# Opening sums added in pairs, the last projection step reordered by bank, the first transposes of attention moved behind one more tile

## The chip, the core and the metric

The kernel runs on one core of one Trainium2 chip. The metric is device time in microseconds of one execution. Three runs of the kernel before gave 907.13, 908.06 and 908.67 us, median 908.06. The core has five engines that run side by side: TensorE (PE in the profile, its weight loads PEld), VectorE (DVE), ScalarE (ACT), GpSimd (POOL) and SyncE (SP, which issues nearly all transfers here).

## What is computed

A trunk of two layers over 512 tokens of 1024 channels, in float32, with a final RMSNorm. Each layer normalises its input, scales and shifts it by values that come from a conditioning vector `c`, mixes tokens, and adds the result back:

```
h = rmsnorm(x, norm_g[i]) * (1.0 + scale) + shift
y = even_mixer(...) if i == 0 else odd_mixer(...)
x = x + (1.0 + gate) * y
```

The change lies in layer 0. There one projection of `h` gives pool channels, `q`, `k`, `v` and a gate. `q`, `k`, `v` feed 16 heads of 64 channels of stick-breaking attention, strictly causal and without a softmax:

```
z = q k^T / 8
log_fail = where(causal, -softplus(z), 0)
after = reverse cumulative sum of log_fail, minus log_fail
a = where(causal, exp(log_sigmoid(z) + after), 0)
o = a v
```

The pool channels go through a causal sliding mean and a small matrix. Both branches are multiplied by SiLU(gate) and projected back.

## The kernel before

**Layout.** Activations lie with channels on the 128 partitions and tokens along the row: `x` is eight tiles of 128x512. Float32 products are made of three passes: each operand is split into a rounded part (`hi`) and a remainder (`lo`), and TensorE adds hi x hi, lo x hi and hi x lo in one PSUM bank (`mm3`, lines 189 to 193). The split is a copy on ScalarE (line 60) and a subtraction on VectorE (line 61). Weights come in units of 512 KB: `load_upto` (line 71) issues their transfers on SyncE into three buffers, `split_upto` (line 78) splits them into three more, and `next_unit` (line 92) hands them out in turn and works two units ahead.

**Banks.** PSUM has eight banks, in two pools: three for projection tiles (`pm`, tile names `m` and `av`) and five for everything else (`pz`, names `z` and `zb`).

**Who orders the work.** For TensorE and SyncE the order of the program text holds throughout (line 498). In `start()` it holds for ScalarE, VectorE and GpSimd too (line 666); elsewhere a scheduler orders those three by readiness and its own costs, and it may put an instruction of later text into a gap of an ordered stretch. It also gives out buffers and banks, by which is free first.

**The opening, `start()` (lines 543 to 660).** Eight matmuls of zeros in bfloat16 (`warm_up(8)`, line 564) are followed by two products of `deps` that start the banks of the token sums with a small constant, and by two products that spread `silu(c)` over the partitions (`cbc`). Then each of the eight `x` tiles is squared, seven on ScalarE and the last on VectorE (lines 574 to 579), and `colsum` (line 142) sums each half of each square over the partitions by a product with ones: 16 sums, each of them two instructions on TensorE. After twelve more warm-up matmuls come the reciprocal root on ScalarE (line 616), its refinement on VectorE (`newton`), and then a loop over the eight channel tiles `k`. In each step VectorE and ScalarE make `hh[k]` and `hl[k]` from `x[k]`, VectorE makes two dot products of `silu(c)` with rows of the conditioning weights (`ada_dot`, line 110, from a ring of four buffers that SyncE refills), the weight unit is split, and TensorE adds to eight banks at once: four of `v` (`pv`, a block of 128 tokens each, lines 656 and 657) and four of `q`, `k` and the first gates (`pq`, lines 658 and 659). A step is three passes over these eight banks:

```
for n, (h, w) in enumerate(((hh, whi), (hl, whi), (hh, wlo))):
    for p, c in zip(pv, tok):
        mm(p, h[:, c], w[:, :512], start=f and n == 0, stop=l and n == 2)
    for p, c in zip(pq, col):
        mm(p, w[:, c], h, start=f and n == 0, stop=l and n == 2)
```

so all eight banks of the last step are complete only near its end.

**After the opening (`layer0`, lines 662 to 681).** `qk_post` (line 313) copies and splits `q` and `k` out of their banks, `v_post` (line 410) does so for `v`, and `silu_ps` (line 210: a sigmoid on ScalarE, a multiply on VectorE) makes the gates `sga` and `sgp`. Each frees its bank. The order of these on ScalarE and VectorE is the scheduler's.

**The loop over pairs of heads (lines 704 to 773).** `self.seq` lists projection tiles (`mtile`, line 195: 24 matmuls of 512 columns): first `u`, then for each later pair `q`, `k`, `ga`, `u`, `gp`. Between the tiles stand the parts of attention of the pair before: `z` (`attn_z`, line 340: scores on TensorE, two sigmoids on ScalarE, masks on GpSimd, scans on VectorE, and one long multiply on VectorE at line 370), `tr` (`attn_t`, line 373: ten transposes on TensorE, then a split), `av` (`attn_av`, line 389: the product with `v`). For the first pair, `u` is followed by `z(0,0)`, the `q` tile by `z(0,1)` and `tr(0,0)`, the `k` tile by `av(0,0)` and `tr(0,1)`, the `ga` tile by `z(1,0)`.

Of the kernel before, what the change touches and what calls it, by code (L numbers as in the profile page):

```python
# [8 lines left out]
F32R = mybir.dt.float32r  # L9
AF = mybir.ActivationFunctionType  # L10
ALU = mybir.AluOpType
# [3 lines left out]
DVE = mybir.EngineType.DVE  # L15
# [22 lines left out]
class Trunk:  # L38
# [504 lines left out]
    def start(self):  # L543
# [15 lines left out]
        def warm_up(n):  # L559

            for _ in range(n):
                mm(warm, self.zero[:, :P], self.zero, start=True, stop=True)

        warm_up(8)

        ps = [self.zbank()[:, :256] for _ in range(2)]
        for p in ps:
# [6 lines left out]
        for k in range(KT):  # L574
            sq = sqs[k // 2][:, k % 2]
            if k == KT - 1:
                nc.vector.tensor_tensor(out=sq, in0=self.x[k], in1=self.x[k], op=ALU.mult)
            else:
                self.square(k, full, sq)
            for p, sl in zip(ps, halves):  # L580
                self.colsum(p, sq[:, sl], False, k == KT - 1)
        warm_up(12)
        nc.sync.dma_start(self.cst, io["cst"])
        ring = self.ap.tile([P, 4, 1024], F32, tag="vs", name="ring")
# [41 lines left out]
        for k in range(KT):  # L626
            self.load_upto(k + 1)
            u = self.units[k]
            whi = self.wp.tile([P, 1024], F32R, tag="whi", name="whi", bufs=3)
            wlo = self.wp.tile([P, 1024], F32R, tag="wlo", name="wlo", bufs=3)  # L630
            if k:
                t = self.h_scale(0, k, rstd, full)
                dot(0, k)
                nc.scalar.copy(out=whi, in_=u["raw"])
                self.h_hi(0, k, t, full)
                dot(1, k + 1)
                self.h_lo(0, k, t, full)
            else:
                self.h_hi(0, 0, t[:, ha], ha)
                nc.scalar.copy(out=whi[:, :512], in_=u["raw"][:, :512])  # L640
                self.h_hi(0, 0, t[:, hb], hb)
                nc.scalar.copy(out=whi[:, 512:], in_=u["raw"][:, 512:])
                self.h_lo(0, 0, t[:, ha], ha)
                self.h_lo(0, 0, t[:, hb], hb)
            nc.vector.tensor_tensor(out=wlo, in0=u["raw"], in1=whi.bitcast(F32), op=ALU.subtract)
            if k == 0:
                dot(1, 1)
            self.split_done = self.used = k + 1
            load(1, k + 2), load(0, k + 2)
            self.load_upto(k + 3)  # L650
            f, l = k == 0, k == KT - 1
            tok = [slice(tb * P, (tb + 1) * P) for tb in range(4)]
            col = [slice(512 + i * P, 512 + (i + 1) * P) for i in range(4)]
            hh, hl = self.hh[k], self.hl[k]
            for n, (h, w) in enumerate(((hh, whi), (hl, whi), (hh, wlo))):
                for p, c in zip(pv, tok):
                    mm(p, h[:, c], w[:, :512], start=f and n == 0, stop=l and n == 2)  # L657
                for p, c in zip(pq, col):
                    mm(p, w[:, c], h, start=f and n == 0, stop=l and n == 2)  # L659
        return pv, pq  # L660

    def layer0(self):
        nc, io = self.nc, self.io
        self.plan_l0()
        self.plan_l1()
        with self.tc.manual_schedule(engines={ACT, DVE, POOL}):
            pv, pq = self.start()
        self.vs = self.ap.tile([P, 4, 1024], F32R, tag="vs", name="vs")

        self.kl = {}  # L670
        for e, z in (("e", slice(64, P)), ("o", slice(0, 64))):
            self.kl[e] = self.ap.tile([P, S], F32R, tag="kl" + e, name="kl" + e)
            nc.vector.memset(self.kl[e][z].bitcast(F32), 0.0)
        self.qk_post(pq[0], "q")
        self.qk_post(pq[1], "k")
        for tb in range(2):
            self.v_post(pv[tb], tb)
        sga = {0: self.silu_ps(pq[2], "sga")}
        for tb in range(2, 4):
            self.v_post(pv[tb], tb)  # L680
        sgp0 = self.silu_ps(pq[3], "sgp")

        self.ada_rest = [(0, 2, k) for k in range(KT)] + [(1, pt, k) for pt in range(3) for k in range(KT)]
        ya, yp, pin, sgp = {}, {}, {}, {self.POOLS[0]: sgp0}
# [2 lines left out]
        def tr(p, par):  # L687
            st["a"] = self.attn_t(st.pop(("s", p, par)))

        def av(p, par):  # L690
            if par == 0:
                st["yt"] = self.t512("yt", bufs=1)
            aps = self.attn_av(2 * p + par, st["a"])
            self.av_post(par, aps, st["yt"])
            if par == 1:
                t = self.t512("t")
                nc.vector.tensor_tensor(out=t, in0=st["yt"], in1=sga.pop(p), op=ALU.mult)
                ya[p] = self.ytile()
                self.hilo(ya[p][0], ya[p][1], t)

        def z(p, par):
            st[("s", p, par)] = self.attn_z(par)

        p = 0
        for kind, j in self.seq:
            if kind == "q":
# [2 lines left out]
                if j == 1:  # L709
                    z(0, 1)  # L710
                self.qk_post(ps, "q")
                tr(j - 1, 0)
            elif kind == "k":
                self.qk_post(self.mtile(), "k")
                av(j - 1, 0)
                tr(j - 1, 1)
            elif kind == "pg":
                yp[2 * j], yp[2 * j + 1] = self.pool_group(
                    j, (pin[2 * j], pin[2 * j + 1]), (sgp[2 * j], sgp[2 * j + 1])
# [2 lines left out]
                    tr(7, 0)  # L722
            elif kind == "ga":
                sga[j] = self.silu_ps(self.mtile(), "sga")
                z(j, 0)
            elif kind == "u":
                pin[j] = self.pool_u(self.mtile(), j)
# [139 lines left out]
def _layout(inp):  # L867
# [11 lines left out]
    sel = np.concatenate([w0[:, :3072], w0[:, 4096:]], axis=1)  # L879
    a["w0m"] = mt(sel, 40)  # L880
    a["w0s"] = np.concatenate(
        [v[:, :512], w0[:, 1024:1152], w0[:, 2048:2176], w0[:, 5120:5248], w0[:, 4864:4992]], axis=1
    ).reshape(KT, P, 1024)
    a["w0v"] = v[:, 512:].reshape(4, 2, P, 512).transpose(0, 2, 1, 3).reshape(4, P, 1024)
    wo = lambda w: w.reshape(16, P, 8, P).transpose(2, 1, 0, 3)
# [39 lines left out]
```

## Time and profile before

| what | value |
|---|---|
| median of three runs | 908.06 us |
| the profiled execution | 907.16 us |
| its span, first to last instruction | 905.5 us |
| mean granted TensorE clock | 0.989 |
| busy: TensorE, its weight loads | 881.9 us (97%), 737.8 us (81%) |
| busy: VectorE, ScalarE, GpSimd | 573.1 us (63%), 354.1 us (39%), 52.1 us (6%) |
| chain that ended last, by engine | TensorE 91%, VectorE 6%, ScalarE 1% |
| memory traffic | 106.69 MB, mean 118 GB/s |

The span leaves out what lies around the first and last instruction. A busy share is a mean over the whole span; the opening, the hand-over to attention and the end have other limits than the long stretch of projection tiles between them. The granted clock is a share of full speed: 1.00 is 2.4 GHz and 0.50 is 1.2 GHz, and a number between them is a stretch with both. A matmul's busy time overlaps with the next one's, so the pace of a row of matmuls is read from their starts.

### The profile page before, as it was taken

The numbers are of one execution on the slowest core, as the hardware profiler recorded it, in microseconds if no ns is written. First come the engines' busy times: TensorE is split into PE (matmuls) and PEld (weight loads), VectorE is DVE, ScalarE is ACT, GpSimd is POOL, SyncE is SP. The second block draws the span as 40 slices with busy tenths as digits, with TensorE's granted clock in tenths as the row PEclk, the third lists the DMA queues.
The fourth block names the chain that finished last, engine by engine and source line by source line (L and its number), as shares of the span: only waits on it lengthen the run. The fifth ranks groups of instructions, "written<-read, shape, count | busy, mean of one in ns | idle before, by whom it ended". The sixth has DMA issues, their size and how long they took to land.

```text
span 905.5 us, 10821 instructions
## 1 busy us (share of the span) xinstructions
PE 881.9 (97%) x4187; PEld 737.8 (81%) x4188; DVE 573.1 (63%) x815; ACT 354.1 (39%) x551; POOL 52.1 (6%) x104
## 2 busy tenths in 40 slices
PE   8988999999999999999999999999999999999995
PEld 5767888888888888888998888888888888888884
DVE  5977889788978688596675445555434444444445
ACT  5355655556322546564443222222112222222331
POOL 0002112012000012020000000000000000000002
PEclk9998999999999999999999999999999999999997
DMA  8851122224677321113512333333332222332202
GB/s 305 282 204 45 39 94 70 82 71 140 227 260 285 100 82 59 59 58 127 165 48 96 129 124 117 117 117 117 104 105 93 93 93 93 101 109 93 93 24 93
DMA packets 30725, 106.69 MB, mean 118 GB/s; under 512 B 3409, under 2 KB 3537, under 8 KB 30674
## 3 DMA queue, kind: packets, MB, share of 16 engines
q1 hardware_dynamic: 30386, 105.48, 34.4%
q8 instruction: 33, 0.54, 0.2%
q10 hardware_dynamic: 288, 0.52, 0.2%
q14 instruction: 18, 0.15, 0.0%
HBM read 103.90 MB, written 2.10 MB: 117 GB/s over the span
## 4 chain that ended last, share of the span: by engine, by line
PE 91%; DVE 6%; ACT 1%; issue 1%; DVEq 0%; POOL 0%; ACTq 0%; POOLq 0%
PE m L191 25%; PE m L192 25%; PE m L193 25%; PE zb L657 2%; PE z L384 2%; PE av L397 2%; PE m L659 2%; PE zb L143 1%; DVE f L368 1%; PE z L354 1%; PE z L353 1%; PE zb L778 1%; PE zb L777 1%; PE zb L779 1%; PE zb L192 1%
## 5 line engine op out<-in xcount | busy, mean ns | idle before, releaser
L60 ACT CAST whi<-raw 128x1024 fp32r<-128x1024 f32 (+1 forms) x137 | 142.8, 1043 | 426.4 <-PE m L192 324.9
L191 PE MATMUL m<-hh,whi 128*128 128x512 f32 x768 | 301.8, 393 | 6.1 <-DVE sga L213 5.5
L192 PE MATMUL m<-hl,whi 128*128 128x512 f32 x768 | 299.9, 391 | 0.0
L193 PE MATMUL m<-hh,wlo 128*128 128x512 f32 x768 | 299.7, 390 | 0.0
L61 DVE TENSOR_TENSOR wlo<-raw,whi 128x1024 fp32r<-128x1024 f32 (+1 forms) x137 | 165.2, 1207 | 124.6 <-ACT whi L60 117.4
L191 PEld LDWEIGHTS m<-hh,whi 128*128 128x128 f32 x768 | 144.9, 189 | 36.2 <-DVE sga L213 5.9
L193 PEld LDWEIGHTS m<-hh,wlo 128*128 128x128 f32 x768 | 144.7, 188 | 30.5
L192 PEld LDWEIGHTS m<-hl,whi 128*128 128x128 f32 x768 | 144.9, 189 | 29.3
L191 PE MATMUL m<-yh,whi 128*128 128x512 f32 (+1 forms) x288 | 105.7, 367 | 0.0
L192 PE MATMUL m<-yl,whi 128*128 128x512 f32 (+1 forms) x288 | 105.3, 365 | 0.0
L193 PE MATMUL m<-yh,wlo 128*128 128x512 f32 (+1 forms) x288 | 105.2, 365 | 0.0
L226 DVE SCALAR_TENSOR_TENSOR x<-m,small,x 128x512 f32<-128x512 f32 (+1 forms) x36 | 24.8, 691 | 64.1 <-PE m L193 64.1
L191 PEld LDWEIGHTS m<-yh,whi 128*128 128x128 f32 x288 | 54.3, 189 | 8.9
L192 PEld LDWEIGHTS m<-yl,whi 128*128 128x128 f32 x288 | 54.3, 189 | 8.8
L193 PEld LDWEIGHTS m<-yh,wlo 128*128 128x128 f32 x288 | 54.3, 189 | 8.7
L362 POOL TENSOR_SCALAR_AFFINE_SELECT s<-s 128x128 f32<-128x128 f32 x64 | 41.3, 668 | 281.5 <-ACT s L357 281.5
L368 DVE TENSOR_TENSOR_SCAN f<-f,mask 128x512 f32<-128x512 f32 (+1 forms) x64 | 52.3, 847 | 0.0
L818 DVE TENSOR_TENSOR u<-m,t 128x512 f32<-128x512 f32 x16 | 11.1, 692 | 56.0 <-PE m L193 49.6
L60 ACT CAST yh<-t 128x512 fp32r<-128x512 f32 x40 | 24.9, 622 | 45.7 <-DVE t L441 20.3
L831 DVE TENSOR_TENSOR t<-t,m 128x512 f32<-128x512 f32 x15 | 10.3, 689 | 50.3 <-PE m L193 50.3
L114 DVE CUSTOM_DVE_ANT_0 araw<-araw,cbc,cst 128x1024 f32<-128x1024 f32 x32 | 40.5, 1278 | 1.9 <-DMA araw<-in_ada 1.8
L61 DVE TENSOR_TENSOR yl<-t,yh 128x512 fp32r<-128x512 f32 x40 | 27.2, 687 | 1.4 <-ACT yh L60 1.4
(177 smaller groups left out, 946.1 us busy)
## 6 DMA issues: line engine op xcount, KB each, us to landing
raw<-in_w1m SPq DMA_DIRECT2D x64, 512.0 KB, 3.3
raw<-in_w0m SPq DMA_DIRECT2D x36, 512.0 KB, 3.3
araw<-in_ada SPq DMA_DIRECT2D x32, 512.0 KB, 4.9
ring<-in_ada SPq DMA_DIRECT2D x16, 512.0 KB, 5.8
raw<-in_w0o SPq DMA_DIRECT2D x16, 512.0 KB, 4.5
raw<-in_w1o SPq DMA_DIRECT2D x16, 512.0 KB, 3.3
raw<-in_w0s SPq DMA_DIRECT2D x8, 512.0 KB, 5.7
x<-in_x SPq DMA_DIRECT2D x8, 256.0 KB, 4.8
```

The lines of the kernel that those rows point to most:

```text
L60: a = self.nc.scalar.copy(out=hi, in_=src)
L61: b = (eng or self.nc.vector).tensor_tensor(out=lo, in0=src, in1=hi.bitcast(F32), op=ALU.subtract)
L114: ins = nc.vector.tensor_tensor_reduce(raw, raw, self.cbc, 1.0, self.cst[:, b : b + 1], ALU.mult, ALU.add, col)
L191: mm(ps, wh, xh, start=first, stop=False)
L192: mm(ps, wh, xl, start=False, stop=False)
L193: mm(ps, wl, xh, start=False, stop=last)
L226: self.nc.vector.scalar_tensor_tensor(x, ps[:, sl], self.adacol(layer, 2, mt), x, ALU.mult, ALU.add)
L362: nc.gpsimd.affine_select(out=sw[:, d], in_=sw[:, d], pattern=[[-1, P]], compare_op=ALU.is_gt, fill=0.0, base=0, channel_multiplier=1,)
L368: nc.vector.tensor_tensor_scan(r, r, self.mask[:, S - n :][:, ::-1], 1.0, ALU.mult, ALU.max)
L384: nc.tensor.transpose(ps[:, do : do + P], sw[:, so : so + P], self.ident)
L397: self.nc.tensor.matmul(ps[:, kb * P :], vs[:, kb, c : c + P], t[:, o : o + w], start=(n == 0 and kb == 0), stop=(n == 1 and kb == 3),)
L657: mm(p, h[:, c], w[:, :512], start=f and n == 0, stop=l and n == 2)
```

## The change

Four edits, and one in the layout of the weights that goes with them.

1. The first warm-up group has four matmuls and not eight.
2. Squares 0 and 1, 2 and 3 are added by GpSimd, squares 4 and 5 by VectorE; TensorE then sums three pairs and the squares 6 and 7 by themselves, 10 sums and not 16.
3. In the last of the eight projection steps the first pass goes over all eight banks, and then the second and third pass of each bank follow one another, in the order gate, gate, `q`, `k`, `v` (banks 5, 6, 4, 7, 0 to 3). The columns of `w0s` are stored so that bank 5 is the pool branch's gate, bank 6 the attention branch's gate and bank 7 `k`. The work behind it (a one-column sigmoid, the split of the weight unit of the next tile, both gates, `q`, `k`, `v`) moves from `layer0` to the end of `start()`, where the order of the text holds on ScalarE and VectorE as well.
4. For the first pair of heads `tr(0,0)` moves from behind the `q` tile to behind the `k` tile, and `av(0,0)` with `tr(0,1)` from behind the `k` tile to behind the `ga` tile, ahead of `z(1,0)`.

```diff
--- before.py
+++ after.py
@@ -561,7 +561,7 @@
             for _ in range(n):
                 mm(warm, self.zero[:, :P], self.zero, start=True, stop=True)
 
-        warm_up(8)
+        warm_up(4)
 
         ps = [self.zbank()[:, :256] for _ in range(2)]
         for p in ps:
@@ -577,8 +577,12 @@
                 nc.vector.tensor_tensor(out=sq, in0=self.x[k], in1=self.x[k], op=ALU.mult)
             else:
                 self.square(k, full, sq)
-            for p, sl in zip(ps, halves):
-                self.colsum(p, sq[:, sl], False, k == KT - 1)
+            if k in (1, 3, 5):
+                two = sqs[k // 2]
+                (nc.vector if k == 5 else nc.gpsimd).tensor_tensor(out=sq, in0=two[:, 0], in1=two[:, 1], op=ALU.add)
+            if k % 2 or k == 6:
+                for p, sl in zip(ps, halves):
+                    self.colsum(p, sq[:, sl], False, k == KT - 1)
         warm_up(12)
         nc.sync.dma_start(self.cst, io["cst"])
         ring = self.ap.tile([P, 4, 1024], F32, tag="vs", name="ring")
@@ -652,33 +656,50 @@
             tok = [slice(tb * P, (tb + 1) * P) for tb in range(4)]
             col = [slice(512 + i * P, 512 + (i + 1) * P) for i in range(4)]
             hh, hl = self.hh[k], self.hl[k]
-            for n, (h, w) in enumerate(((hh, whi), (hl, whi), (hh, wlo))):
-                for p, c in zip(pv, tok):
-                    mm(p, h[:, c], w[:, :512], start=f and n == 0, stop=l and n == 2)
-                for p, c in zip(pq, col):
-                    mm(p, w[:, c], h, start=f and n == 0, stop=l and n == 2)
-        return pv, pq
+
+            def product(bank, h, w, n):
+                if bank < 4:
+                    mm(pv[bank], h[:, tok[bank]], w[:, :512], start=f and n == 0, stop=l and n == 2)
+                else:
+                    mm(pq[bank - 4], w[:, col[bank - 4]], h, start=f and n == 0, stop=l and n == 2)
+
+            passes = ((hh, whi), (hl, whi), (hh, wlo))
+            if l:
+
+                order = (5, 6, 4, 7, 0, 1, 2, 3)
+                for bank in order:
+                    product(bank, *passes[0], 0)
+                for bank in order:
+                    product(bank, *passes[1], 1)
+                    product(bank, *passes[2], 2)
+            else:
+                for n, (h, w) in enumerate(passes):
+                    for bank in range(8):
+                        product(bank, h, w, n)
+
+        nc.scalar.activation(self.junk, self.eps, AF.Sigmoid)
+        self.split_upto(KT + 1)
+        sgp = self.silu_ps(pq[1], "sgp")
+        sga = self.silu_ps(pq[2], "sga")
+        self.vs = self.ap.tile([P, 4, 1024], F32R, tag="vs", name="vs")
+        self.qk_post(pq[0], "q")
+        self.qk_post(pq[3], "k")
+        for tb in range(4):
+            self.v_post(pv[tb], tb)
+        return sga, sgp
 
     def layer0(self):
         nc, io = self.nc, self.io
         self.plan_l0()
         self.plan_l1()
-        with self.tc.manual_schedule(engines={ACT, DVE, POOL}):
-            pv, pq = self.start()
-        self.vs = self.ap.tile([P, 4, 1024], F32R, tag="vs", name="vs")
 
         self.kl = {}
         for e, z in (("e", slice(64, P)), ("o", slice(0, 64))):
             self.kl[e] = self.ap.tile([P, S], F32R, tag="kl" + e, name="kl" + e)
             nc.vector.memset(self.kl[e][z].bitcast(F32), 0.0)
-        self.qk_post(pq[0], "q")
-        self.qk_post(pq[1], "k")
-        for tb in range(2):
-            self.v_post(pv[tb], tb)
-        sga = {0: self.silu_ps(pq[2], "sga")}
-        for tb in range(2, 4):
-            self.v_post(pv[tb], tb)
-        sgp0 = self.silu_ps(pq[3], "sgp")
+        with self.tc.manual_schedule(engines={ACT, DVE, POOL}):
+            sga0, sgp0 = self.start()
+        sga = {0: sga0}
 
         self.ada_rest = [(0, 2, k) for k in range(KT)] + [(1, pt, k) for pt in range(3) for k in range(KT)]
         ya, yp, pin, sgp = {}, {}, {}, {self.POOLS[0]: sgp0}
@@ -709,11 +730,15 @@
                 if j == 1:
                     z(0, 1)
                 self.qk_post(ps, "q")
-                tr(j - 1, 0)
+                if j > 1:
+                    tr(j - 1, 0)
             elif kind == "k":
                 self.qk_post(self.mtile(), "k")
-                av(j - 1, 0)
-                tr(j - 1, 1)
+                if j > 1:
+                    av(j - 1, 0)
+                    tr(j - 1, 1)
+                else:
+                    tr(0, 0)
             elif kind == "pg":
                 yp[2 * j], yp[2 * j + 1] = self.pool_group(
                     j, (pin[2 * j], pin[2 * j + 1]), (sgp[2 * j], sgp[2 * j + 1])
@@ -722,6 +747,9 @@
                     tr(7, 0)
             elif kind == "ga":
                 sga[j] = self.silu_ps(self.mtile(), "sga")
+                if j == 1:
+                    av(0, 0)
+                    tr(0, 1)
                 z(j, 0)
             elif kind == "u":
                 pin[j] = self.pool_u(self.mtile(), j)
@@ -879,7 +907,7 @@
     sel = np.concatenate([w0[:, :3072], w0[:, 4096:]], axis=1)
     a["w0m"] = mt(sel, 40)
     a["w0s"] = np.concatenate(
-        [v[:, :512], w0[:, 1024:1152], w0[:, 2048:2176], w0[:, 5120:5248], w0[:, 4864:4992]], axis=1
+        [v[:, :512], w0[:, 1024:1152], w0[:, 4864:4992], w0[:, 5120:5248], w0[:, 2048:2176]], axis=1
     ).reshape(KT, P, 1024)
     a["w0v"] = v[:, 512:].reshape(4, 2, P, 512).transpose(0, 2, 1, 3).reshape(4, P, 1024)
     wo = lambda w: w.reshape(16, P, 8, P).transpose(2, 1, 0, 3)
```

## Rows read from the trace of the kernel before

**Rows 1.** The cores: span and mean granted TensorE clock.
```profile
core 0: 905.5 us, clock 0.989
```

**Rows 2.** Waits of TensorE, whole run: line, releaser, us in total, times, longest.
```profile
PE m L191 <- DVE sga L213: 5.5, 1, 5.5
PE z L384 <- DVE s L370: 1.9, 1, 1.9
...
PE zb L657 <- ACT whi L640: 1.5, 1, 1.5
PE av L397 <- DVE al L61: 0.9, 1, 0.9
```

**Rows 3.** Windows: length, busy by engine (instructions), granted clock, DMA share, GB/s.
```profile
64.10:69.60 5.50, 0.01 (x1) 0.01 (x1) 5.27 (x9) 5.35 (x11) 0.00 (x0) 0.70 0.31 101
69.60:73.20 3.60, 3.60 (x9) 2.84 (x10) 2.71 (x6) 2.12 (x6) 0.00 (x0) 0.51 0.00 0
64.10:101.30 37.20, 29.68 (x131) 24.80 (x132) 31.00 (x47) 23.42 (x46) 6.72 (x9) 0.86 0.17 51
101.30:104.50 3.20, 3.20 (x18) 2.73 (x17) 0.00 (x0) 1.09 (x2) 0.00 (x0) 1.00 0.00 0
86.90:90.30 3.40, 3.40 (x14) 3.16 (x15) 3.40 (x6) 2.12 (x5) 2.05 (x4) 0.52 0.37 104
104.50:240.00 135.50, 135.50 (x663) 114.68 (x663) 115.89 (x162) 76.46 (x136) 20.07 (x36) 1.00 0.28 92
```

**Rows 4.** Timeline of the opening, TensorE: start us, us, what, count, idle before.
```profile
1.53 3.53 PE L562 MATMUL zb<-zero 128*128 128x512 bf16 x8 [1.53 <-POOL zero L480]
4.89 1.03 PE L568 MATMUL zb<-deps,ones 128*128 128x256 f32 x4
5.85 1.98 PE L571 MATMUL m<-crow,ones 1*128 1x512 f32 x4
7.76 7.17 PE L143 MATMUL zb<-sq,ones 128*128 128x256 f32 x32
14.77 2.75 PE L562 MATMUL zb<-zero 128*128 128x512 bf16 x11
...
19.00 1.54 PE L657 MATMUL zb<-whi,hh 128*128 128x512 f32 x4 [1.47 <-ACT whi L640]
```

**Rows 5.** The same timeline, ScalarE and VectorE.
```profile
4.95 1.13 ACT L139 ACTIVATE sq<-x 128x512 f32<-128x512 f32 x2
...
7.33 2.58 ACT L139 ACTIVATE sq<-x 128x512 f32<-128x512 f32 x4 [0.41 <-DMA x<-in_x]
...
9.91 0.69 DVE L577 TENSOR_TENSOR sq<-x 128x512 f32<-128x512 f32 x1 [1.35 <-DMA x<-in_x]
...
12.91 0.16 DVE L120 SCALAR_TENSOR_TENSOR small<-small,cst 128x1 f32<-128x1 f32 x1
14.54 0.39 ACT L616 ACTIVATE u<-zb 128x256 f32<-128x256 f32 x1 [4.62 <-PE zb L143]
```

**Rows 6.** Line 860 on GpSimd: duration in ns, shortest, median, longest.
```profile
L860 POOL TENSOR_TENSOR o<-x,u x8: 720/902/942, 891.6 to 900.1; 128x256 f32<-128x256 f32 x8
```

**Rows 7.** Timeline, last step of the opening and the first pair of heads.
```profile
58.49 1.07 PE L657 MATMUL zb<-whi,hh 128*128 128x512 f32 x4
...
63.25 0.84 PE L659 MATMUL m<-hh,wlo 128*128 128x512 f32 x3
...
66.93 1.28 ACT L212 ACT_TABLE_LOAD   x1
...
68.22 0.60 ACT L212 ACTIVATE sga<-m 128x512 f32<-128x512 f32 x1
...
68.85 0.69 DVE L213 TENSOR_TENSOR sga<-sga,m 128x512 f32<-128x512 f32 x1
...
85.25 1.48 DVE L370 TENSOR_TENSOR s<-s,f 128x1279 f32<-128x1279 f32 x1
...
103.44 0.39 PE L353 MATMUL z<-khe,qe 128*128 128x512 f32 x1
```

## The prediction

> **What bounds the kernel now.** I read the span first: 905.5 us between the first and last instruction [rows 1], while the profiled execution took 907.16 us and the median of the three runs is 908.06. My sum is made against 907.16 and then moved up by the 0.90 between the two. The mean granted clock beside it is 0.989, so TensorE runs at half speed only for short stretches; in the table of the profile it is also the engine that is busy for nearly all of the span. The time is then what TensorE streams plus the time it stands or runs at half speed, and the next view is its own list of waits [rows 2]. Two waits are in reach of the change: 5.5 us before the first projection tile after the opening, which waits for VectorE's multiply of `sga`, and 1.9 us before the first transpose of attention, which waits for VectorE's multiply at L370. The 1.5 us before the opening's first projection and the 0.9 us before the first `av` are smaller.
>
> Then the windows [rows 3]. The reader should look at the clock column. Idle for 5.5 us, TensorE then runs from 69.6 to 73.2 at a granted clock of 0.51, that is at 1.2 GHz in place of 2.4; after the second wait it runs from 86.9 to 90.3 at 0.52. A wait there is paid twice. Three of the windows say where VectorE stands: 31.0 us of work in the 37.2 us up to 101.3, then 3.2 us with nothing to do, and 115.89 of 135.5 us (86%) busy afterwards.
>
> **The opening sums.** Now 16 column sums run as 32 instructions in 7.17 us, 0.224 us each, from 7.76 to 14.93 without a gap [rows 4]. The squares that feed them were ready earlier: ScalarE's last at 9.91, VectorE's at 10.60 [rows 5]. TensorE is the bound here. Six sums (12 instructions, 12 x 0.224 = 2.7 us) go away, but three adds come in, and two of them lie on GpSimd.
>
> Nothing in this trace adds 128x512 on GpSimd. The nearest row is its multiply of 128x256, 0.72 us at its shortest and 0.94 at its longest, beside a busy VectorE [rows 6]. The low end for the add is 0.72 (all of it fixed cost), the high end 2 x 0.94 = 1.88. I take 2 x 0.72 = 1.44, because VectorE is almost idle at that time. The third add, on VectorE, costs the 0.69 of the same shape [rows 5].
>
> Follow the steps. The first two squares end at 4.95 + 1.13 = 6.08, the pair at 7.52, and its four sum instructions (0.90) at 8.42. The fourth square ends at 7.33 + 2.58/4 = 7.98, its pair at 9.42, its sums at 10.32. Square 5 ends at 9.27 and VectorE's add at 9.96, under that cover; sums to 11.22. Square 6 is alone: 12.12. Square 7 now stands behind the add on VectorE and ends at 10.65, still covered. The first half of its sums ends at 12.12 + 0.45 = 12.57. Today it ends at 14.93 - 0.45 = 14.48, and ScalarE takes it at 14.54 [rows 5]. Gain 1.9 us. With a 0.72 us add, VectorE's pair at 9.96 rules and the gain is 2.3; with 1.88 it is 1.5. What is late next is VectorE's first dot product, which ends at 12.91 + 0.16 = 13.07 because its DMA landed late [rows 5]; the new chain wants VectorE at 12.57 + 0.9 = 13.5, so the gain cannot pass about 2.3.
>
> The Trainium skill, GPSIMD Engine Reference, section "Engine selection", speaks against this placement: it sends elementwise adds to VectorE and calls GpSimd about two times slower. With all three adds on VectorE at its own 0.69 the gain would come out at 2.3 instead of 1.9, so the rule is worth 0.4 us here.
>
> Four warm-up matmuls less (4 x 0.44 = 1.8 us, [rows 4]) let the `deps` sums and the two `crow` products begin earlier. I cost this at nothing: they then wait for `crow` or for the first pair, and the copies of `cbc` are not on the path. The projection's first step still waits for `whi` after the second warm-up group; its 1.5 us [rows 2] stay, since the whole chain to it moves together. The loads behind it are issued when VectorE's dot products free the ring, which move too; the queue on SyncE loses and gains no issue.
>
> **The last step of the opening.** From 58.49 to 63.25 there are 21 matmuls, 0.2267 us each [rows 7]; the step has 24 and ends at 64.09. The reorder changes no count. Under the new order the first gate bank is complete after 8 + 2 matmuls, that is 2.27 us into a step that begins at 58.49 - 1.9 = 56.6: at 58.9. ScalarE's sigmoid takes 0.60 and VectorE's multiply 0.69, so the bank is free at about 60.2. The table load of 1.28 us, today at 66.93, is moved ahead of it by the one-column sigmoid, into a stretch where ScalarE is idle; should it not be, 61.5 is still before the step ends at 62.2. So the next tile finds a free bank and the whole 5.5 us goes. With no idle stretch in front, the 3.6 us at 0.51 go as well: 3.6 x 0.49 = 1.8 us.
>
> In the fixed order the `q`, `k` and `v` copies stand behind both gates on ScalarE and VectorE. The copies are needed only by the scores of attention, after a tile of 24 x 0.2267 = 5.4 us, at 67.7. VectorE has 5.27 + 2.71 = 8.0 us of such work in the two windows [rows 3]; begun at 59.6 it ends at 67.6. The banks that the scores take first (`q`, then the first `v` banks) are free before that. The split of the eighth weight tile is pinned ahead of the gates; its load is already issued, and it costs nothing. The columns of the weights are only stored in another order.
>
> **Attention one tile later.** No instruction is added and no DMA moves; the first head's transposes, and its `av` with the second head's transposes, each go behind one more tile. Today TensorE arrives 1.9 us before L370 ends at 85.25 + 1.48 [rows 2, 7]. A tile of 5.4 us more in between leaves 3.5 us of room. The wait goes, and with it 3.4 x 0.48 = 1.6 us of half clock [rows 3]. Between first transpose and first `av` there is still one tile, with VectorE as loaded as before, so I leave the 0.9 us there [rows 2].
>
> **The sum.** 1.9 + 5.5 + 1.8 + 1.9 + 1.6 = 12.7 us. 907.16 - 12.7 = 894.5, and with the 0.9 to the median **895.4 us**.
>
> **The rivals.**
> *The wait moves to VectorE (0.20).* Its 31.0 us of work begin at 59.6 and, without a gap, end at 90.6. TensorE reaches the scores of the next pair, today at 103.44 [rows 7], at 103.44 - 12.7 = 90.7. There is no reserve, where today there are 3.2 us. Against a large loss speaks that the second head's transposes need only part of that work. If one wait of the old size returns with its half clock: 895.4 + 3.5 = 898.9.
>
> *The opening gives nothing (0.08).* If a GpSimd add takes T, the second pair is ready at 6.08 + 2T, and the gain is zero at T = 2.6 us, well above the 1.88. Then 897.3.
>
> *The opening runs at half clock (0.07).* The first eight warm-up matmuls take 0.44 us each, the later eleven 0.25 [rows 4]: the first group streams at the lower level although the column reads 1.00. With half of them gone and gaps before the pairs, the sums might stream at that level: five groups at 1.79 us end their critical part 3.1 us later, at 15.7, and the time is 898.5. Against it: TensorE is busy from 1.53 on all the same, and the 1.5 us idle before the first projection cost no clock. The Trainium skill, TensorE: Matmul & The Clock Gate, section "What's actually happening", says that the throttled state is the default and activity releases it; by that rule the shorter warm-up is a risk, and the present trace agrees with its start.
>
> *The bank is not free after all (0.05).* If the order of slots gives the next tile a bank that is emptied last, up to 5.5 + 1.8 stay: 902.7.
>
> *Slower: VectorE stays behind for good (0.04).* If it never recovers the lost reserve, each later pair meets the old wait with its half clock, 3.5 us. Four pairs (14 us) eat the 12.7; with six the time is 895.4 + 21 = 916.4. It decides from the fourth pair on. Against it: VectorE's 86% after 104.5 leaves 19.6 us.
>
> The forecast itself has 0.56.
>
> **Range and chances.** Downward: 0.4 from a fast GpSimd add, 0.9 if the `av` wait goes, and 0.7 of spread among the runs: 893.4. Upward it holds the three middle rivals, and the first two together: 898.9 + 1.9 = 900.8. About 0.2% (1.8 us) is what a measurement can tell from no change; only the last rival is slower, and little of the others' tails reaches the band around no change: faster 0.93, same 0.03, slower 0.04.
>
> **What would show it.** ScalarE's first reciprocal root near 12.6 instead of 14.54; no TensorE wait for `sga` or `sgp`; the granted clock at 1.00 from 60 on; the first transpose without a wait. A wait at L384 or L397 of over a microsecond, with a clock near 0.5 behind it, would show the first rival; sums 0.45 us apart the third. The forecast is wrong if TensorE's waits up to 110 add up to more than some 6 us.

## The result, and the profile after

The changed kernel takes 896.91 us (median of four runs, 896.37 to 897.56), the kernel before 907.71 us beside it: a ratio of 0.988, 95% interval 0.9863 to 0.9897. That is 10.8 us less; 895.4 was forecast, with 893.4 to 900.8 as the range. The profiled executions went from 907.16 to 897.10 us, their spans from 905.5 to 895.4: 10.1 us, where the sum of the prediction, made against the profile, had 12.7.

TensorE's waits come first again. The list of the changed kernel, to be laid beside [rows 2]:

```profile
PE zb L143 <- ACT u L139: 1.9, 1, 1.9
...
PE zb L662 <- ACT whi L644: 1.5, 1, 1.5
PE z L353 <- DVE al L61: 1.3, 1, 1.3
PE av L397 <- DVE al L61: 0.9, 1, 0.9
PE zb L143 <- POOL sq L582: 0.7, 1, 0.7
```

The 5.5 us for `sga` and the 1.9 us for L370 are gone. Two lines are new: 1.3 us before scores of attention (L353), and 0.7 us for a pair of squares from GpSimd.

The timeline of the opening, TensorE, GpSimd and ScalarE:

```profile
1.53 1.89 PE L562 MATMUL zb<-zero 128*128 128x512 bf16 x4 [1.53 <-POOL zero L480]
...
6.22 1.26 POOL L582 TENSOR_TENSOR sq<-sq 128x512 f32<-128x512 f32 x1 [4.18 <-ACT sq L139]
...
7.54 6.53 PE L143 MATMUL zb<-sq,ones 128*128 128x256 f32 x20 [0.70 <-POOL sq L582]
...
8.00 1.27 POOL L582 TENSOR_TENSOR sq<-sq 128x512 f32<-128x512 f32 x1 [0.51 <-ACT sq L139]
...
13.67 0.39 ACT L620 ACTIVATE u<-zb 128x256 f32<-128x256 f32 x1 [3.83 <-PE zb L143]
...
18.12 1.54 PE L662 MATMUL zb<-whi,hh 128*128 128x512 f32 x4 [1.47 <-ACT whi L644]
```

Twenty sum instructions take 6.53 us where 20 x 0.224 = 4.5 was due [rows 4]. The windows of the same stretch tell why (columns as in [rows 3]):

```profile
5.00:8.00 3.00, 2.30 (x6) 0.96 (x7) 1.38 (x2) 2.40 (x5) 1.27 (x2) 1.00 1.01 324
8.30:11.40 3.10, 2.96 (x8) 1.88 (x7) 1.36 (x2) 1.51 (x3) 0.96 (x1) 0.50 1.05 414
11.50:13.60 2.10, 2.10 (x11) 1.84 (x11) 1.45 (x3) 0.00 (x0) 0.00 (x0) 1.00 1.03 421
```

From 8.3 to 11.4 the granted clock is 0.50, that is 1.2 GHz. It falls at 8.0, when the sums of the first pair are under way, behind the wait of 0.70 us for that pair (6.84 to 7.54); the wait for the second pair, 0.14 us, already lies in the half clock. Eleven matmuls fall into the 2.1 us after it, eight into the 3.1 us of it (those cut by an edge counted).

The hand-over to attention, in the timeline of the changed kernel:

```profile
60.11 0.60 ACT L212 ACTIVATE sgp<-m 128x512 f32<-128x512 f32 x1 [1.51 <-PE m L664]
...
60.74 0.69 DVE L213 TENSOR_TENSOR sgp<-sgp,m 128x512 f32<-128x512 f32 x1 [0.70 <-ACT sgp L212]
...
63.08 0.39 PE L191 MATMUL m<-hh,whi 128*128 128x512 f32 x1
...
68.52 0.39 PE L353 MATMUL z<-khe,qe 128*128 128x512 f32 x1
...
81.98 1.25 PE L384 MATMUL z<-ident,s 128*128 128x128 f32 x10
...
91.42 0.48 PE L353 MATMUL z<-khe,qe 128*128 128x512 f32 x1
...
94.00 0.39 PE L353 MATMUL z<-khe,qe 128*128 128x256 f32 x1 [1.34 <-DVE al L61]
...
94.34 0.40 PE L191 MATMUL m<-hh,whi 128*128 128x512 f32 x1
```

and the places of the kernel before that belong to them and are not among its rows above:

```profile
69.59 0.79 PE L191 MATMUL m<-hh,whi 128*128 128x512 f32 x1 [5.50 <-DVE sga L213]
...
76.80 0.39 PE L353 MATMUL z<-khe,qe 128*128 128x512 f32 x1
...
104.70 0.40 PE L191 MATMUL m<-hh,whi 128*128 128x512 f32 x1
```

The gate's bank is free at 60.74 + 0.69 = 61.4, and the next tile starts at 63.08, straight behind the step. From these starts the time can be told by stretch:

| stretch, from the start of one to the start of the next | before | changed | won |
|---|---|---|---|
| the first instruction to the first projection | 19.00 | 18.12 | 0.88 |
| to the first tile after the opening | 50.59 | 44.96 | 5.63 |
| to the scores of the first pair | 7.21 | 5.44 | 1.77 |
| to the scores of the second pair | 26.64 | 22.90 | 3.74 |
| to the tile behind them | 1.26 | 2.92 | -1.66 |
| to the end | 800.8 | 801.1 | -0.3 |

The middle three rows are what was forecast (5.5, 1.8, and 1.9 + 1.6). The first is 1.0 short of its 1.9, and the fifth was not in the sum. The experiments ask about these two, and about what in the last step did the work.

### The profile page after: what moved, and what is told of

Its sections match the earlier page's. It is cut to its first block, busy times and chain, and to the rows that moved or that the text cites. A ratio compares the mean times of both kernels' runs of the same rounds, so it can differ in the third digit from the quotient of the medians.

```text
span 895.4 us, 10797 instructions
## 1 busy us (share of the span) xinstructions
PE 877.2 (98%) x4172; PEld 733.9 (82%) x4172; DVE 573.8 (64%) x816; ACT 353.5 (39%) x552; POOL 56.4 (6%) x106
## 4 chain that ended last, share of the span: by engine, by line
PE 90%; DVE 6%; ACT 1%; issue 1%; DMA 1%; SPq 0%; POOL 0%; DVEq 0%; ACTq 0%
PE m L191 25%; PE m L192 25%; PE m L193 25%; PE zb L662 2%; PE av L397 2%; PE m L664 2%; PE z L384 1%; DVE f L368 1%; PE zb L143 1%; PE z L353 1%; PE zb L806 1%; PE zb L805 1%; PE zb L807 1%; PE z L354 1%; PE zb L191 1%
## 5 line engine op out<-in xcount | busy, mean ns | idle before, releaser
L362 POOL TENSOR_SCALAR_AFFINE_SELECT s<-s 128x128 f32<-128x128 f32 x64 | 43.2, 698 | 270.2 <-ACT s L357 252.4
L859 DVE TENSOR_TENSOR t<-t,m 128x512 f32<-128x512 f32 x15 | 10.3, 688 | 50.3 <-PE m L193 50.3
L845 POOL MEMSET u<- 128x16 f32 x16 | 1.8, 112 | 423.3 <-DVE t L854 347.5
```

The lines of the kernel that those rows point to most:

```text
L362: nc.gpsimd.affine_select(out=sw[:, d], in_=sw[:, d], pattern=[[-1, P]], compare_op=ALU.is_gt, fill=0.0, base=0, channel_multiplier=1,)
```

## The experiments

All ratios are to the kernel before, run beside each set: 908.29 us for the first four, 908.11 for the next four, 908.19 for the last three.

**1. The gaps filled.** Zeros are multiplied while TensorE would wait for the first and the second pair.

```diff
                 nc.vector.tensor_copy(self.cbc[:, i * 512 : (i + 1) * 512], pc[i])
+        warm_up(3)
...
+            if k == 1:
+                warm_up(4)
```

> The changed kernel, with three warm-up matmuls more between the crow products and the first pair of squares and four more between the first and the second pair. Theory A (the opening won only 0.87 us because TensorE's clock fell to 0.50 behind the gaps it waits in for the pairs): the granted clock stays at 1.00 through the sums, ScalarE's first reciprocal root moves from 13.67 to about 12.6, the first projection from 18.12 to about 17.1, and the time from 896.9 to about 895.9. Theory B (the hand-over of the pairs themselves takes that long, the clock only fills waiting time): the root stays near 13.6 and the time at 896.9.

Measured: a median of 899.62 us, ratio 0.9907 (0.989 to 0.9923), but not as one value: the profiled execution took 895.80, the three others 899.60 to 899.90. In the profiled one the clock holds and theory A's numbers nearly come out:

```profile
9.72 3.62 PE L143 MATMUL zb<-sq,ones 128*128 128x256 f32 x16
...
12.95 0.38 ACT L623 ACTIVATE u<-zb 128x256 f32<-128x256 f32 x1 [2.95 <-PE zb L143]
...
17.40 1.54 PE L665 MATMUL zb<-whi,hh 128*128 128x512 f32 x4 [1.47 <-ACT whi L647]
```

Sixteen sums take 3.62 us, 0.226 each, the root comes at 12.95 and the projection at 17.40. So in that execution filling the gaps kept the clock and brought the root 0.7 us ahead of the changed kernel's, seven extra matmuls included. What the other three lost 4 us to is not known, as only this one has a profile. All four have the same mean granted clock, 0.996, so it is no fall that the clock's record shows; the next run suggests another cause.

**2. No pairs, short warm-up kept.**

```diff
-            if k in (1, 3, 5):
...
-            if k % 2 or k == 6:
-                for p, sl in zip(ps, halves):
+            for p, sl in zip(ps, halves):
```

> The changed kernel without the pairs: 16 sums as before the change, behind the four warm-up matmuls. Theory A: the sums start at about 6.85, where the crow products end, run without a gap at 0.224 us each for 7.17 us and end at about 14.0, so the root stays near 13.6 and the time at 896.9; the shorter warm-up alone then brought what the opening won. Theory B (the pairs brought the 0.87 us): the root goes back to about 14.5 and the time rises by 0.9 to 897.8.

Measured: 901.37 us, ratio 0.9926 (0.9911 to 0.994), all four between 901.17 and 901.73. Neither theory has it: the root comes at 17.53, four microseconds late.

```profile
5.05 3.78 PE L571 MATMUL m<-crow,ones 1*128 1x512 f32 x4
8.76 9.17 PE L143 MATMUL zb<-sq,ones 128*128 128x256 f32 x32
```

Two windows of the sums alone (busy time of TensorE and of its weight loads, clock, DMA share, GB/s):

```profile
10.00:11.00 1.00, 1.00 (x3) 0.79 (x3) 1.00 0.99 406
...
14.00:15.00 1.00, 1.00 (x7) 0.87 (x6) 1.00 1.02 414
```

The `crow` products take 3.78 us in place of 1.98 [rows 4], and three matmuls touch the microsecond at 10 where six or seven do from 13 on. TensorE streams at half pace until about 13, without a gap, while the column reads 1.00. The trace itself says why: its first record of the clock, a rise to the full level, stands at 12.8 us, and the column reads 1.00 ahead of it for want of a record. There the spacing of the instructions is what counts. Against run 4, which differs in the warm-up alone, this run is 3.4 us slower.

**3. Eight warm-up matmuls, pairs kept.**

```diff
-        warm_up(4)
+        warm_up(8)
```

> The changed kernel with eight warm-up matmuls again, pairs kept. Theory A (the clock falls where TensorE stands between sums): the crow products end at 7.8 and the first pair is waiting by then, so one gap is gone and the one before the second pair is left; the clock falls less or not at all, and the root comes at 12.6 to 13.0; time 895.9 to 896.3. Theory B (the shorter warm-up is what let the sums begin early): the root goes back to 14.5, the time to 897.8.

Measured: 895.85 us, ratio 0.9867 (0.9852 to 0.9882). The root comes at 13.05:

```profile
8.86 4.58 PE L143 MATMUL zb<-sq,ones 128*128 128x256 f32 x20
```

Here no pair is waited for, twenty sums take 4.58 us, and though they begin 1.3 us later than in the changed kernel they end 0.6 us earlier. Theory A: it is the clock that was given away behind the gap. That not even the second pair is waited for has another source: in this profile the first rise of the clock comes at 7.2 us and the `crow` products end at 8.9, not at the expected 7.8. The profiles of runs 6, 7, 8 and 10 have the same opening, waits of 0.17 to 0.39 us among the sums, and no fall there. The difference in time is 1.1 us; the two intervals overlap, and one of the four times here, 897.26, lies among the changed kernel's.

**4. Eight warm-up matmuls, no pairs** (edits 2 and 3 together: the opening as it was before the change, all else changed).

> Eight warm-up matmuls and 16 sums, as before the change; all else as changed. Against the run with eight warm-up matmuls and pairs (895.85, first reciprocal root at 13.05). Theory A (the pairs save six sums on TensorE, the bound there, as long as the clock holds): the root comes at 14.5 to 15.6, by when the clock rises, and the time at 897.3 to 898.4. Theory B (the pairs save nothing, they trade sums for waits): root at 13.5 or earlier, time within 0.4 of 895.9.

Measured: 897.99 us, ratio 0.989 (0.9873 to 0.9908); root at 14.83, sums in 7.17 us:

```profile
8.05 7.17 PE L143 MATMUL zb<-sq,ones 128*128 128x256 f32 x32
```

Theory A. With eight warm-up matmuls the pairs are worth 897.99 - 895.85 = 2.1 us (each against its own neighbours: 0.989 against 0.9867 of 908 us is 2.1 too). The changed kernel's whole opening, pairs and short warm-up together, is worth about 0.7 to 1.1 by this run (896.91 and, below, 897.34), which is within the intervals.

**5. The order of attention undone.**

```diff
-                if j > 1:
-                    tr(j - 1, 0)
+                tr(j - 1, 0)
...
-                if j > 1:
-                    av(j - 1, 0)
-                    tr(j - 1, 1)
-                else:
-                    tr(0, 0)
+                av(j - 1, 0)
+                tr(j - 1, 1)
...
-                if j == 1:
-                    av(0, 0)
-                    tr(0, 1)
                 z(j, 0)
```

> The changed kernel with the first pair's transposes and products where they were before the change (one tile earlier). Theory A (the order of attention removed the wait for L370 and its half clock, 3.5 us, and brought in a wait of 1.3 us before the next pair's scores): a wait of about 1.9 us at the first transposes comes back, with a granted clock near 0.5 behind it, the wait of 1.3 us goes, and the time rises by about 2.2 us to 899.1. Rival (VectorE's whole work up to there sets the time, whatever the order): waits add up to the same, time 896.9 within 0.5.

Measured: 900.03 us, ratio 0.9916 (0.99 to 0.9932). The profile is of the longest of the four executions, 902.60 us, whose first reciprocal root comes at 16.05, 2.4 us later than the changed kernel's; so stretches are compared and not whole times. TensorE's timeline and one window:

```profile
70.89 0.39 PE L353 MATMUL z<-khe,qe 128*128 128x512 f32 x1
...
80.96 1.28 PE L384 MATMUL z<-ident,s 128*128 128x128 f32 x10 [1.92 <-DVE s L370]
...
89.70 1.48 PE L397 MATMUL av<-al,vs 128*128 128x512 f32 x4 [1.41 <-DVE al L61]
90.97 2.36 PE L384 MATMUL z<-ident,s 128*128 128x128 f32 x10
...
99.13 0.39 PE L353 MATMUL z<-khe,qe 128*128 128x512 f32 x1
```
```profile
92.00:95.00 3.00, 3.00 (x13) 2.66 (x12) 2.42 (x5) 2.59 (x5) 0.00 (x0) 0.63 0.24 87
```

The old wait is back to the hundredth, 1.92 us. The half clock is back too, though one wait later, behind the `av` (0.50 from 90.8 to 94.2; the window mixes it with the full level). From the scores of the first pair to those of the second it takes 28.24 us against 22.90: 5.3 more, of which the wait ahead of the next tile gives 1.66 back. That is 3.7 us by the stretch; the medians differ by 2.7 to 3.1, with the opening's spread (below) in them. Theory A, then, with 1.5 us more than it had; the rival's sum of waits does not stay the same.

**6. The old order of the last step, gates still first behind it** (on top of eight warm-up matmuls, as the two after it, so that the opening is steadier).

```diff
-            if l:
...
-            else:
-                for n, (h, w) in enumerate(passes):
-                    for bank in range(8):
-                        product(bank, h, w, n)
+            for n, (h, w) in enumerate(passes):
+                for bank in range(8):
+                    product(bank, h, w, n)
```

> Pairs and eight warm-up matmuls; the last projection step goes pass by pass over the eight banks again, but the work behind it keeps its fixed order with the gates first. Theory A (the place of the gates in ScalarE's and VectorE's order carries most of the 5.5 us; the order of the banks carries the rest): the first gate's bank is complete at the 22nd of 24 matmuls, sigmoid and multiply free it about 1.2 us after the step ends, so TensorE waits 1.0 to 1.4 us, keeps its clock, and the time is 897.1. Theory B (the order of the banks carries it): a wait of 4 us or more with half clock behind it, time 901 or more.

Measured: 899.21 us, ratio 0.9899 (0.9881 to 0.9917), single times 897.58 to 899.80, against 895.85 with the new order.

```profile
62.51 1.23 DVE L61 TENSOR_TENSOR wlo<-raw,whi 128x1024 fp32r<-128x1024 f32 x1 [3.96 <-PE m L664]
...
63.66 0.68 DVE L213 TENSOR_TENSOR sgp<-sgp,m 128x512 f32<-128x512 f32 x1
...
64.39 0.50 PE L191 MATMUL m<-hh,whi 128*128 128x512 f32 x1 [1.97 <-DVE sgp L213]
```

TensorE waits 1.97 us, not 1.0 to 1.4: the scheduler has put the split of a later weight unit (1.23 us) ahead of the gate's multiply on VectorE. And the clock does not hold:

```profile
66.00:69.00 3.00, 3.00 (x8) 2.30 (x7) 1.72 (x3) 1.88 (x5) 0.00 (x0) 0.50 0.06 22
```

From the first tile to the scores it now takes 7.17 us where run 3 takes 5.44: the half clock costs another 1.7. The time lies between the two theories (897.1, and 901 or more). Theory A in kind, but not in size: with the gates first, 2.0 of the 5.5 us are left, and nearly all of the half clock.

**7. The new order of the last step, the work behind it left to the scheduler again** (moved back to `layer0`, outside the stretch in which the order of the text holds).

```diff
-        nc.scalar.activation(self.junk, self.eps, AF.Sigmoid)
-        self.split_upto(KT + 1)
-        sgp = self.silu_ps(pq[1], "sgp")
...
+        self.qk_post(pq[0], "q")
+        self.qk_post(pq[3], "k")
...
+        sgp0 = self.silu_ps(pq[1], "sgp")
```

> Pairs and eight warm-up matmuls; the last step keeps the order by banks with the gates first, but the work behind it is left to the scheduler again, without the early sigmoid. Theory A (once a gate's bank is complete 3 us before the step ends, it is taken first in any order): the table load of 1.28 us comes behind the complete bank, the bank is free at about 3.0 us after it is complete, near the end of the step, TensorE waits 0 to 0.5 us, time 895.9 to 896.4. Theory B (the fixed order is what frees the bank): a wait of 3 us or more with half clock behind it, time 900 or more.

Measured: 895.92 us, ratio 0.9866 (0.9851 to 0.9882), the same as with the fixed order.

```profile
56.54 1.28 ACT L212 ACT_TABLE_LOAD   x1
...
59.50 0.60 ACT L212 ACTIVATE sgp<-m 128x512 f32<-128x512 f32 x1 [1.68 <-PE m L664]
...
62.47 0.39 PE L191 MATMUL m<-hh,whi 128*128 128x512 f32 x1
```

There is no wait at all, less than theory A allowed: the table load is over at 57.82, ahead of the bank, which ScalarE waits for until 59.50. Completing the gate's bank early is enough; the fixed order behind it and the early sigmoid add nothing that can be measured here.

**8. Scores ahead of the second transposes.**

```diff
                 if j == 1:
                     av(0, 0)
-                    tr(0, 1)
                 z(j, 0)
+                if j == 1:
+                    tr(0, 1)
```

> Pairs and eight warm-up matmuls; behind the gate tile of the second pair the scores of that pair go ahead of the first pair's second transposes. Theory A (the 1.3 us wait before those scores is a shortage of banks: three of five are held by the transposes until VectorE has split them): the wait goes, time 894.5. Theory B (VectorE has no reserve at that point, whoever holds the banks): a wait of about the same size comes at the transposes or at the product behind them, time within 0.5 of 895.9.

Measured: 894.77 us, ratio 0.9854 (0.9838 to 0.987).

```profile
89.43 0.45 PE L353 MATMUL z<-khe,qe 128*128 128x512 f32 x1
...
90.76 1.04 PE L384 MATMUL z<-ident,s 128*128 128x128 f32 x8
92.12 0.44 PE L384 MATMUL z<-ident,s 128*128 128x128 f32 x2 [0.32 <-ACT s L357]
92.31 0.48 PE L191 MATMUL m<-hh,whi 128*128 128x512 f32 x1
```

Theory A: the same work in another order leaves 0.32 us of the 1.34. All four times, 894.64 to 895.15, lie below those of run 3. The new wait was one for banks. Transposes take three of the five banks of their pool and hold them until VectorE has split them: in the changed kernel the first is free 3.6 us after the transposes begin (90.39 to 94.00). Scores take three too, but here ScalarE has emptied the first of them after 2.7 us (89.43 to 92.12).

**9. The changed kernel once more, in one set with the two after it.**

> The changed kernel once more, in one set with the next two. Theory A (with four warm-up matmuls the moment at which TensorE reaches 2.4 GHz differs from execution to execution, and the sums of the opening take it in full): single times spread over 2 us or more, between 896 and 901, and the sums of the profiled one start or run at half pace somewhere. Theory B (the opening is as steady as before): all times within 896.4 to 897.6 as in the first set.

Measured: 897.34 us, ratio 0.9881 (0.9864 to 0.9897); single times 896.45, 896.47, 898.21 and 898.75, so the spread is there, and the profiled one is among the long ones:

```profile
9.27 6.51 PE L143 MATMUL zb<-sq,ones 128*128 128x256 f32 x16 [0.58 <-POOL sq L582]
...
15.39 0.39 ACT L620 ACTIVATE u<-zb 128x256 f32<-128x256 f32 x1 [5.56 <-PE zb L143]
```
```profile
8.60:14.80 6.20, 5.62 (x14) 4.45 (x14) 2.82 (x5) 1.19 (x3) 0.62 (x1) 0.50 1.03 412
```

The same program, and now the half clock lasts at least 6.2 us and the root comes later than in the kernel before, 15.39 against 14.54 [rows 5].

**10. Eight warm-up matmuls and scores first, timed again.**

> Eight warm-up matmuls, pairs, and the scores of the second pair ahead of the first pair's second transposes, as in the run that measured 894.77: 894.3 to 895.3 in every execution if the opening is steady with eight, and 1.5 to 3 us under the changed kernel of the same set.

Measured: 894.99 us, ratio 0.9856 (0.9842 to 0.9871), all four between 894.77 and 895.25; 2.35 us under the changed kernel beside it. This beats both kernels. Its sums wait too, but less than the changed kernel's, and the clock does not fall among them. What is left in its opening stands in one window, behind TensorE's 1.5 us wait for the first projection:

```profile
9.20 3.90 PE L143 MATMUL zb<-sq,ones 128*128 128x256 f32 x16 [0.39 <-POOL sq L582]
```
```profile
19.00:21.00 2.00, 2.00 (x6) 1.51 (x6) 1.97 (x4) 0.37 (x1) 0.00 (x0) 0.50 0.92 365
```

**11. All three adds on VectorE**, on top of that.

```diff
-                (nc.vector if k == 5 else nc.gpsimd).tensor_tensor(out=sq, in0=two[:, 0], in1=two[:, 1], op=ALU.add)
+                nc.vector.tensor_tensor(out=sq, in0=two[:, 0], in1=two[:, 1], op=ALU.add)
```

> The same with all three adds of squares on VectorE (0.69 us each) in place of two on GpSimd (1.26 us each). Theory A (the sums wait for the pairs): the second pair is ready 0.5 us earlier, the root comes 0.1 to 0.5 us earlier, time 894.4 to 894.8. Theory B (TensorE's start behind the crow products or the last squares set the root): root and time the same within 0.2.

Measured: 897.94 us, ratio 0.9889 (0.9874 to 0.9903): 2.95 us slower, which neither theory had.

```profile
8.95 0.69 DVE L572 COPY cbc<-m 128x512 f32<-128x512 f32 x1 [0.17 <-PE m L571]
9.56 1.89 DVE L582 TENSOR_TENSOR sq<-sq 128x512 f32<-128x512 f32 x3
```
```profile
10.29 6.27 PE L143 MATMUL zb<-sq,ones 128*128 128x256 f32 x20 [1.38 <-DVE sq L582]
```

In the order of the text the copies of `cbc`, which wait for TensorE's `crow` products, stand on VectorE ahead of the adds. The squares of the first pair are ready at 6.12, but the three adds run one behind another from 9.56; TensorE waits 1.38 us, and its clock falls (0.54 from 10.3 to 13.9). A part of the loss may have another source: in this profile the clock's first rise comes at 7.2 us, against 4.7 in run 10's, and the `crow` products end 1.2 us later, which has nothing to do with the adds. The parts were not separated, and adds on VectorE ahead of the copies were not run.

## Why the prediction was right, point by point

**The last step (5.5 + 1.8 forecast, 5.63 + 1.77 measured).** Right, and for the reason given: the gate's bank is free before the step ends (61.4 and 63.1 measured, 60.2 and 62.2 forecast). Of the two parts of the edit the order of the banks does it alone (run 7); the fixed order alone leaves 1.97 us and a half clock (run 6).

**Attention one tile later (1.9 + 1.6 forecast, 3.74 measured).** Right; undoing it brings the wait back at 1.92 us (run 5). That a wait is paid twice is no fixed sum: in run 5 the half clock came behind another wait than before.

**The opening sums (1.9 forecast, 0.88 in one profile and -0.85 in the other).** This term was mis-sized, and the step that failed is the sentence against the rival of the half clock: that TensorE is busy anyway, and that 1.5 us of idling cost no clock before. The prices of the steps held: the GpSimd add took 1.27 us between the bounds of 0.72 and 1.88 (1.44 was taken), the pairs were ready at 7.48 and 9.27 (7.52 and 9.42 forecast), the sums took 0.224 to 0.229 us each at full pace. But behind the wait for the first pair, 0.70 us in one execution and 0.46 in the other, came a fall to 0.50, for at least 3.1 us in the one and 6.2 in the other. That the gap and not the short warm-up alone brings it, run 11 shows, which has eight warm-up matmuls, a gap of 1.38 us and the same fall. Nor was the 1.5 us wait good evidence: it stands in all thirteen profiles, and in four of them (runs 2, 6, 7 and 10) some 3 us at 0.50 follow it. The rival had a chance of 0.07 and a price of 3.1 us; it came in part, at 1.0 to 2.8 us. The Trainium skill, TensorE: Matmul & The Clock Gate, section "What's actually happening", says that activity lifts the throttle and the default is the lower level; 0.50 behind the gaps of runs 9 and 11, and 0.229 us for each sum of run 3, which had no gap, agree with it. Run 2 does not: there TensorE is busy from 1.52 us on and still streams at half pace until about 13, and the measurement decides.

**"I cost this at nothing", of the four warm-up matmuls.** Wrong, and by the clock again. Eight of them with the pairs are about 1.2 us better (0.9867 against 0.988, with intervals that overlap), though they start the sums 1.3 us later. Without the pairs the difference is clear: 897.99 us with eight (run 4) and 901.37 with four (run 2), where TensorE stays at half pace to about 13 us.

**No wait for VectorE (0 forecast, 1.66 measured in that stretch).** The first rival, at 0.20, came at less than half its price of 3.5 us: 1.34 us and no fall of the clock. Its place was named rightly, the scores of the next pair, but its cause was not VectorE's work alone: run 8 has the same work and 0.32 us of wait. The sum had counted VectorE's time and not who holds the banks meanwhile.

**The other rivals.** The bank was free, the adds were not too slow, and VectorE did catch up: from 94.3 to 240 TensorE is busy without a gap.

```profile
94.30:240.00 145.70, 145.70 (x707) 123.07 (x706) 123.63 (x181) 78.93 (x143) 21.99 (x36) 1.00 0.32 110
```

**The adds on GpSimd.** The rule of the Trainium skill, GPSIMD Engine Reference, section "Engine selection", is right about the engines here (1.27 us against 0.69 for the same add), and at this place of the text it was the wrong choice: run 11 obeys it and is 2.95 us slower, with the adds behind copies that waited for TensorE. The 0.4 us that the prediction gave it was costed from durations, without what stands ahead on the engine.

**The signs.** TensorE's waits up to 110 add up to 5.6 us, under the 6 that would have spoken against the forecast. That sign could not show what went wrong in the opening, which was half clock more than waiting; the root did, at 13.67 and 15.39 where 12.6 was named. The granted clock is 1.00 from 60 on, up to 885 us, and the first transposes do not wait, as forecast.

**Two slips in the range.** The 0.9 us before an `av` [rows 2] is not at the first one: the list is of the whole run, and the wait stands at 403 us in the kernel before (0.89) and at 393 in the changed one (0.88). The first `av`, at 95.07 and 88.56, waits for nothing, so the 0.9 us in the lower end of the range had no base there. And the upper end, 900.8, does not hold the rival of the bank, which was priced at 902.7.

In sum 12.7 was forecast and 10.1 measured between the two profiles: -1.0 in the opening, -1.7 at the scores, +0.3 in the stretches between, and -0.3 behind them. That the medians are nearer, 895.4 and 896.91, is luck: the 0.9 added between profile and median did not come, the profiled execution of the changed kernel being 0.2 above its median.

## What to carry to other kernels

Where several products fill several banks at once, finish first the bank that the next tile needs; the order of the last pass cost nothing here, and a scheduler takes what is ready first. When sums are thinned out so that TensorE waits for their inputs, look at its clock before counting the saving: fewer instructions with gaps between them can end later than more without. An add can belong to the engine that is free at that moment, even if that engine takes twice as long for it; and a reordered use of a bank pool is costed by who empties the banks, not by the work alone.

## What the runs showed of the hardware that had not been expected

The granted clock reads 1.00 from the first instruction on, also where the spacing shows half pace: 0.44 us per warm-up matmul against 0.25 [rows 4], and three matmuls in a microsecond at 10 us in run 2. In every trace here the first record of the clock is a rise to the full level, and the column knows nothing ahead of it.

The moment at which TensorE first reaches full pace is not fixed: by the spacing of the instructions and by the first record it lies near 5 us in the profiles of the kernel before and of the changed one, near 7 in run 3, and near 13 in run 2. In run 3 this cost little: its root comes at 13.05, that of run 10, with the rise at 4.7, at 12.71. The spread of 2.3 us among the executions of the changed kernel (run 9) is another thing as far as its profile tells: there the rise comes at 4.7 and the loss is the fall among the sums. Run 1's three executions at 899.6 to 899.9 beside one at 895.8 fit a late rise, but none of the three has a profile, so this stays open, as does what decides the moment.
